# Low halves by an accumulating DMA, a single pace for the modulation items, and another filler among the attention heads

## The chip, the cores and the metric

One core of a Trainium2 chip runs one program. The time is what the device takes for one execution, in microseconds (us); the median of three runs is given. Engines are called as in the profile: PE (TensorE), PEld (its weight loads), DVE (VectorE), ACT (ScalarE), POOL (GpSimd) and SP (SyncE, which only issues DMAs here). Each engine runs its own list of instructions in order and waits at semaphores.

## What is computed

Two sequences (a prompt and a sample) of 512 tokens with D = 1024 go through the same two layers. Layer 0 mixes by retention (4 heads, scores with a decay in both directions, a gate), layer 1 by grouped-query attention (8 query heads, 2 key heads); each has an MLP of width 4096 with a squared ReLU. A conditioning vector gives six modulation vectors for each layer.

```
def adaln(c, w, b):
    mod = silu(c) @ w + b
    return split(mod, 6)                      # sh1, sc1, g1, sh2, sc2, g2

def trunk(x, c, ...):
    for i in range(2):
        sh1, sc1, g1, sh2, sc2, g2 = adaln(c, mod_w[i], mod_b[i])
        h = rmsnorm(x, norm1_g[i]) * (1 + sc1) + sh1
        m = retention(h, ...) if i == 0 else attention(h, ...)
        x = x + g1 * m
        h = rmsnorm(x, norm2_g[i]) * (1 + sc2) + sh2
        x = x + g2 * (square(relu(h @ mlp_w1[i])) @ mlp_w2[i])
    return rmsnorm(x, final_g)
```

All is fp32. mod_w is 1024 x 6144 in each layer.

## The kernel before

**Products.** A matmul operand in fp32 is split into two halves of the type f32r: hi is the value rounded, lo is the value less hi. `mm3` (L217 to 220) makes a product of three matmuls, hi·hi, hi·lo and lo·hi. Weights come in pieces of 128 x 1024 (512 KB).

**Plain pieces.** `load_piece` (L199 to 207) loads a piece into `raw` on SP's DMA queue (2 buffers), lets ACT copy it into `whi` (L205) and DVE write `wlo` as raw less whi (L206). There are 4 buffers each of whi and wlo. 174 pieces go this way: 128 in the retention (0 to 1000 us of the profiled execution), 46 in the attention (1590 to 2030 us). The two MLPs (1000 to 1590 and 2030 to 2664 us) use products of sums of blocks with their own pieces, and neither `load_piece` nor the modulation.

**Modulation.** The vectors mod are made on DVE, beside the main work. An item is one row block of mod_w for one of six chunks: two loads of 256 KB on POOL's queue (L407) and, for each sequence, two dots on DVE (L382), each a product with a running sum over 512 columns. `bg` holds items not yet loaded, `loaded` those whose loads are issued. `piece` calls `tick` after each plain piece with the instruction that the dots are to stand behind: the pace is added up, and at 1.0 one item is dotted and the next loaded. The items' tiles come from the pool f2 with 8 buffers; 6 of them are held by other things (tables of the rotation, the conditioning rows of the two sequences), so that one item with its two halves fills what is left. With `alt`, every second item takes its tiles from another pool (xf). Only the first 8 items use it before. 40 further dots, on tiles loaded by SP or with `alt`, stand ahead of these.

**Retention.** Eight steps, two sequences with four heads each; in a step PE makes scores, v, g and y, and the q, k products of the next step, in an order written out by hand (`ORDER`). Before, the first 8 items run in step 0, 16 (of one sequence) from the end of step 0 at PACE 0.55, and 8 of one sequence and 72 of both from the end of step 2 at PACE_LAST 1.0, with loops at the ends of steps 3 and 6 and a flush in step 7 that dot what has to be done by then.

**Start.** PE multiplies the first pieces while POOL computes `decay_logs` (L421 on: eleven pairs of small operations, L434 and L435, and three more) and then products for the first norm (L1174).

**Attention.** `weave` runs the heads of a sequence and takes filler from a generator `fill`, a piece at each yield: projections (p1, q2, q0) and the next sequence's norm (`nm1.steps(4)`).

Of the kernel before, what the change touches and what calls it, by code (L numbers as in the profile page):

```python
# [7 lines left out]
F32 = mybir.dt.float32  # L8
# [3 lines left out]
AF = mybir.ActivationFunctionType  # L12
ALU = mybir.AluOpType
# [5 lines left out]
EPS = 1e-6  # L19
ORDER_FIRST = "q0 q1 z0 q2 z1 z2 q3 z3"  # L20
ORDER = "g1 g2 g3 q0 z0 q1 z1 q2 z2 z3 q3"
PACE = 0.55
PACE_LAST = 1.0
SQ_W = 8
SQ_RAW = 3
SQ_SUM = 4
# [5 lines left out]
def kernel(  # L32
# [25 lines left out]
    nc = tc.nc  # L58
    act = nc.scalar.activation
    tt = nc.vector.tensor_tensor  # L60
# [6 lines left out]
    def ld(dst, src):  # L67
        ins = nc.sync.dma_start(dst, src)
        if strict[0]:
            tc.keep_in_program_order(ins)  # L70
        ld.last = ins
# [18 lines left out]
    def rtile():  # L90
        return rp.tile([P, T], F32R, tag="r", name="r")
# [39 lines left out]
    def small(w):  # L131
        return sm.tile([P, w], F32, tag=f"s{w}", name=f"s{w}")
# [13 lines left out]
    bg, loaded = [], []  # L146
    pace = [0.0, 0.0]

    def bg_dot():
        if loaded:  # L150
            f, hv = loaded.pop()
            f(hv)

    def bg_load():
        if bg:
            f, g = bg.pop(0)
            loaded.append((g, f()))

    def tick(ins):
        pace[1] += pace[0]  # L160
# [4 lines left out]
            pace[1] -= 1.0  # L165

    def flush():
        while bg or loaded:
            bg_dot()
            bg_load()  # L170

    sq = {}

# [26 lines left out]
    def load_piece(src):  # L200
        raw = rawp.tile([P, 1024], F32, tag="raw", name="raw")
        ld(raw, src)
        hi = wp.tile([P, 1024], F32R, tag="whi", name="whi")
        lo = wp.tile([P, 1024], F32R, tag="wlo", name="wlo")
        act(hi, raw, AF.Copy)  # L205
        ins = tt(lo, raw, hi.bitcast(F32), ALU.subtract)  # L206
        return hi, lo, ins

    def piece2(src, pages):
# [185 lines left out]
    def new_col(layer, ch, s):  # L395
        modc[layer, ch, s] = const.tile([P, KD], F32, name=f"mc{layer}_{ch}_{s}")

    def mod_chunk(cb, layer, ch, seqs=(0, 1), alt=False):
        accs = {s: small(2 * KD) for s in seqs}
        for s in seqs:  # L400
            new_col(layer, ch, s)

        def load(k):
            get = xtile if alt and k % 2 else f2tile
            hv = [get(), get()]
            for hf in range(2):
                nc.gpsimd.dma_start(hv[hf], modw[layer, ch * KD + k][:, hf * T:(hf + 1) * T])  # L407
            return hv

        def step(k, hv):  # L410
            for s in seqs:
                dot(accs[s], hv, cb[s], k)
            if k == KD - 1:
                for s in seqs:
                    mod_cols(accs[s], layer, ch, s, 0, KD)

        for k in range(KD):
            bg.append((lambda k=k: load(k), lambda hv, k=k: step(k, hv)))

# [677 lines left out]
    def run(g, n=None):  # L1099
        while n is None or n > 0:  # L1100
            try:
                next(g)
            except StopIteration:
                return
            if n is not None:
                n -= 1
# [15 lines left out]
    cb = [cond_row(0), None]  # L1122
# [32 lines left out]
    for i in range(4):  # L1155
        for t in range(2):
            k = 2 * i + t
# [13 lines left out]
            else:  # L1171
# [5 lines left out]
                hi, lo = rtile(), rtile()  # L1177
# [39 lines left out]
    for step in range(8):  # L1217
        s, n = divmod(step, 4)
        nm = None
        r.scores(n, strip)  # L1220
        if step == 3:
            with tc.issue_after(first_pool.ins):
                s1 = stats_of(fetch(xs[1][k]) for k in range(KD))
            nm = Norm(s1, lambda k: fetch(xs[1][k]),
                      modc[0, 1, 1], modc[0, 0, 1], True)
            r1 = Ret(1, None, nm.h)
        if step == 7:
            nm = Norm(stats_of(fetch(park[0][k]) for k in range(KD)), lambda k: fetch(park[0][k]),
                      modc[0, 4, 0], modc[0, 3, 0], True, keep=hparks[0][0])
            m.h[0] = nm.h  # L1230
        if step > 0:
            r.v(n)
        if nm is not None:
            nm.a()
        r.g(n, [0] if step else [3])
        if nm is not None:
            nm.c()
        r.y(n)
        if nm is not None:
            nm.m()  # L1240
        if step < 7:
            strip = decay_strip((n + 1) % 4)
        if step == 7:
            r.g(n, [1, 2, 3])
        if step < 7:
            nxt = r1 if step == 3 else r
            n1 = (n + 1) % 4
            for t in (ORDER if step else ORDER_FIRST).split():
                i = int(t[1])
                if t[0] == "q":  # L1250
                    nxt.qk(n1, i)
                elif t[0] == "z":
                    r.tz([i])
                else:
                    r.g(n, [i])
            if step == 0:
                flush()
                mod_chunk(cb, 0, 1, (1,))
                mod_chunk(cb, 0, 0, (1,))
                pace[0] = PACE  # L1260
            if step == 2:
                flush()
                mod_chunk(cb, 0, 2, (1,))
                for ch in (4, 3, 5):
                    mod_chunk(cb, 0, ch)
                for ch in (1, 0, 2, 3, 4, 5):
                    mod_chunk(cb, 1, ch)
                pace[0] = PACE_LAST
            if step == 3:
                while len(bg) > 71 or (loaded and len(bg) == 72):  # L1270
                    bg_dot()
                    bg_load()
            if step == 6:
                while len(bg) > 47 or (loaded and len(bg) == 48):
                    bg_dot()
                    bg_load()
            if step == 3:
                r.out(n, lambda o: nc.gpsimd.dma_start(park[0][o], x0[o]))
                r1.x = [fetch(xs[1][k], ptile) for k in range(KD)]
                r = r1  # L1280
            else:
                r.out(n)
        else:
            m.x[1] = r.x
            m.ups(0, 0, [0])
            r.tz([0, 1])
            m.ups(0, 0, [1])
            r.tz([2, 3])
            m.ups(0, 0, [2])
            st1 = Stats()  # L1290
            r.out(n, lambda o: st1.add(r.x[o]))
            with tc.issue_after(r.last.ins):
                m.x[0] = [fetch(park[0][k], ftile, nc.scalar) for k in range(KD)]
            m.ups(0, 0, [3])
            flush()
# [30 lines left out]
    nm1 = Norm(st[1], lambda k: fetch(park[1][k]), modc[1, 1, 1], modc[1, 0, 1], True)  # L1326
    a1 = Att(1, nm1.h, tabs)
    p2, p0, p1 = a0.proj(2), a0.proj(0), a0.proj(1)
# [19 lines left out]
    run(zipped(p0, p1))  # L1348

    def fill():  # L1350
        yield from p1
        yield from nm1.steps(4)
        yield from part(q2, 4)
        yield from zipped(q2, q0)

    f = fill()
    weave(a0.heads(), f)
    run(f)
# [20 lines left out]
    f = fill()  # L1379
# [21 lines left out]
    f = finish(0, st[0])  # L1401
# [159 lines left out]
```

## Time and profile before

| | us |
|---|---|
| median of 3 runs | 2667.32 |
| lowest, highest | 2665.93, 2669.35 |
| the profiled execution | 2666.18 |
| its span in the trace | 2664.4 |

The mean granted clock of PE in the profiled execution is 0.981. By stretch, PE's idle time is the length less its busy time: 23.5 us from 0 to 150, 6.8 from 150 to 430, 55.2 from 430 to 1000, 9.4 from 1000 to 1590, 20.3 from 1590 to 2030 and 20.0 to the end. A row of a timeline gives start and length; lengths of neighbours overlap, so the cost of an instruction on its engine is read from one start to the next.

### The profile page before, as it was taken

The numbers are of one execution on the slowest core, as the hardware profiler recorded it, in microseconds if no ns is written. First come the engines' busy times: TensorE is split into PE (matmuls) and PEld (weight loads), VectorE is DVE, ScalarE is ACT, GpSimd is POOL, SyncE is SP. The second block draws the span as 40 slices with busy tenths as digits, with TensorE's granted clock in tenths as the row PEclk, the third lists the DMA queues.
The fourth block names the chain that finished last, engine by engine and source line by source line (L and its number), as shares of the span: only waits on it lengthen the run. The fifth ranks groups of instructions, "written<-read, shape, count | busy, mean of one in ns | idle before, by whom it ended". The sixth has DMA issues, their size and how long they took to land. (4 is left out here: it accounts for less than half of the span.)

```text
span 2664.4 us, 32643 instructions
## 1 busy us (share of the span) xinstructions
PE 2528.7 (95%) x11186; PEld 2056.7 (77%) x11186; DVE 1991.8 (75%) x3800; ACT 1120.2 (42%) x1949; POOL 526.2 (20%) x947
## 2 busy tenths in 40 slices
PE   6999999889897999999999999899999999999998
PEld 4888887767676777888878887678778788878887
DVE  6767577778877978666778867776876766688777
ACT  3433333222222355444444434675774444454432
POOL 2302112221212212121222200000014121242100
PEclk9999999999998999999999999899999999999999
DMA  7544454644444656444565434122337454474433
GB/s 248 190 127 138 126 168 148 205 143 146 134 150 132 210 181 213 163 154 163 171 211 164 162 114 140 53 63 76 115 122 271 157 180 144 160 277 159 139 95 103
DMA packets 133994, 414.00 MB, mean 155 GB/s; under 512 B 21250, under 2 KB 24194, under 8 KB 133828
## 3 DMA queue, kind: packets, MB, share of 16 engines
q0 software_dynamic: 68352, 224.58, 24.9%
q1 hardware_dynamic: 59284, 180.32, 21.6%
q10 hardware_dynamic: 6192, 7.02, 0.8%
q8 instruction: 88, 1.44, 0.2%
q14 instruction: 78, 0.64, 0.1%
HBM read 332.15 MB, written 79.69 MB: 155 GB/s over the span
## 5 line engine op out<-in xcount | busy, mean ns | idle before, releaser
L218 PE MATMUL pm<-r,whi 128*128 128x512 f32 x768 | 306.7, 402 | 29.8 <-DVE f L572 14.6
L205 ACT ACTIVATE whi<-raw 128x1024 fp32r<-128x1024 f32 x174 | 183.6, 1057 | 339.1 <-DMA raw<-in_wri_dram 106.4
L220 PE MATMUL pm<-r,wlo 128*128 128x512 f32 x768 | 304.6, 397 | 9.1 <-DVE wlo L206 9.1
L219 PE MATMUL pm<-r,whi 128*128 128x512 f32 x768 | 305.6, 398 | 5.5 <-DVE r L313 5.4
L382 DVE SCALAR_TENSOR_TENSOR junk<-f,f 128x512 bf16<-128x512 f32 x344 | 239.6, 696 | 94.1 <-DMA f<-in_modw_dram 91.0
L206 DVE TENSOR_TENSOR wlo<-raw,whi 128x1024 fp32r<-128x1024 f32 x174 | 216.9, 1247 | 89.6 <-ACT whi L205 89.0
L225 ACT ACTIVATE wh<-rawq 128x512 fp32r<-128x512 f32 x228 | 142.5, 629 | 286.6 <-PE pm L667 159.7
L225 ACT ACTIVATE wh<-sum 128x512 fp32r<-128x512 f32 x208 | 129.9, 629 | 280.0 <-PE pa L667 178.2
L666 PE MATMUL pa<-r,wh 128*128 128x512 f32 x624 | 242.7, 389 | 0.0
L667 PE MATMUL pa<-r,wh 128*128 128x512 f32 x624 | 242.7, 389 | 0.0
L668 PE MATMUL pa<-r,wh 128*128 128x512 f32 x624 | 242.7, 389 | 0.0
L407 POOL DMA_DIRECT2D f<-in_modw_dram x200 | 108.2, 541 | 596.6 <-DVE junk L382 495.8
L218 PEld LDWEIGHTS pm<-r,whi 128*128 128x128 f32 x768 | 147.3, 192 | 65.0 <-issue 15.9
L666 PE MATMUL pm<-r,wh 128*128 128x512 f32 x468 | 182.6, 390 | 1.9 <-ACT wh L225 1.9
L668 PE MATMUL pm<-r,wh 128*128 128x512 f32 x468 | 182.1, 389 | 0.0
L667 PE MATMUL pm<-r,wh 128*128 128x512 f32 x468 | 182.1, 389 | 0.0
L220 PEld LDWEIGHTS pm<-r,wlo 128*128 128x128 f32 x768 | 147.7, 192 | 42.2 <-DVE wlo L206 11.2
L218 PE MATMUL pa<-whi,r 128*128 128x512 f32 x440 | 174.2, 399 | 5.1 <-ACT whi L205 4.2
L219 PEld LDWEIGHTS pm<-r,whi 128*128 128x128 f32 x768 | 147.9, 193 | 39.8 <-DVE r L313 8.7
L219 PE MATMUL pa<-wlo,r 128*128 128x512 f32 x440 | 174.0, 396 | 0.6 <-DVE wlo L206 0.6
L226 DVE TENSOR_TENSOR wh<-sum,wh 128x512 fp32r<-128x512 f32 x208 | 141.4, 685 | 44.1 <-ACT wh L225 42.7
L220 PE MATMUL pa<-whi,r 128*128 128x512 f32 x440 | 173.6, 394 | 0.0
(277 smaller groups left out, 5978.8 us busy)
## 6 DMA issues: line engine op xcount, KB each, us to landing
rawq<-in_w_dram SPq DMA_DIRECT2D x144, 512.0 KB, 3.9
f<-in_modw_dram POOLq DMA_DIRECT2D x200, 256.0 KB, 3.4
raw<-in_wri_dram SPq DMA_DIRECT2D x92, 512.0 KB, 3.8
r<-hhpark POOLq DMA_DIRECT2D x142, 256.0 KB, 4.1
hhpark<-f POOLq DMA_DIRECT2D x96, 256.0 KB, 2.9
hhpark<-p POOLq DMA_DIRECT2D x88, 256.0 KB, 2.3
raw<-in_wro_dram SPq DMA_DIRECT2D x32, 512.0 KB, 3.7
xf<-park POOLq DMA_DIRECT2D x48, 256.0 KB, 3.4
```

What stands on the lines that cost most here:

```text
L205: act(hi, raw, AF.Copy)
L206: ins = tt(lo, raw, hi.bitcast(F32), ALU.subtract)
L218: mm(ps, a[0], b[0], start=first, stop=False)
L219: mm(ps, a[0], b[1], start=False, stop=False)
L220: return mm(ps, a[1], b[0], start=False, stop=last)
L225: split.last = act(hi, src_f32, AF.Copy)
L226: split.dve = tt(lo, src_f32, hi.bitcast(F32), ALU.subtract)
L382: stt(junk, w[hf], 0.5, cb[hf], ALU.mult, ALU.mult, accum_out=a[:, 2 * k + hf:2 * k + hf + 1])
L407: nc.gpsimd.dma_start(hv[hf], modw[layer, ch * KD + k][:, hf * T:(hf + 1) * T])
L666: mm(ps, a[0], b[0], start=first and k == 0, stop=False, **more)
L667: mm(ps, a[0], b[1], start=False, stop=False, **more)
L668: mm(ps, a[1], b[0], start=False, stop=k == n - 1, **more)
```

## The change

Lines of the kernel after are 3 higher than those of before from L208 on (L206 is then L208 and L209, L382 is L385, L407 is L410, L434 is L437).

- `load_piece`: ACT writes −hi into wlo (the copy with scale −1), and a DMA on POOL's queue adds the piece from DRAM to it. The dots of `tick` stand behind the second copy of ACT.
- `bg_load` loads a second item ahead where its tiles are of another home than the loaded one's; dots take the oldest. `alt` is set for 32 items of layer 1.
- From the end of step 0 all 96 items run at one pace of 0.88. `bg_until(n)` dots until n items are left: 80 in step 2, 72 in step 3, 48 in step 6.
- The first filler in the attention runs p1 and the norm side by side, four yields for both, where they took their turns one after the other.

```diff
--- before.py
+++ after.py
@@ -19,8 +19,7 @@
 EPS = 1e-6
 ORDER_FIRST = "q0 q1 z0 q2 z1 z2 q3 z3"
 ORDER = "g1 g2 g3 q0 z0 q1 z1 q2 z2 z3 q3"
-PACE = 0.55
-PACE_LAST = 1.0
+PACE = 0.88
 SQ_W = 8
 SQ_RAW = 3
 SQ_SUM = 4
@@ -148,13 +147,18 @@
 
     def bg_dot():
         if loaded:
-            f, hv = loaded.pop()
+            f, hv, _ = loaded.pop(0)
             f(hv)
 
     def bg_load():
-        if bg:
-            f, g = bg.pop(0)
-            loaded.append((g, f()))
+        while bg and (not loaded or (len(loaded) == 1 and loaded[0][2] != bg[0][2])):
+            f, g, home = bg.pop(0)
+            loaded.append((g, f(), home))
+
+    def bg_until(n):
+        while len(bg) + len(loaded) > n:
+            bg_dot()
+            bg_load()
 
     def tick(ins):
         pace[1] += pace[0]
@@ -165,9 +169,7 @@
             pace[1] -= 1.0
 
     def flush():
-        while bg or loaded:
-            bg_dot()
-            bg_load()
+        bg_until(0)
 
     sq = {}
 
@@ -203,7 +205,8 @@
         hi = wp.tile([P, 1024], F32R, tag="whi", name="whi")
         lo = wp.tile([P, 1024], F32R, tag="wlo", name="wlo")
         act(hi, raw, AF.Copy)
-        ins = tt(lo, raw, hi.bitcast(F32), ALU.subtract)
+        ins = act(lo, raw, AF.Copy, scale=-1.0)
+        nc.gpsimd.dma_start(lo, src, accum_op=ALU.add)
         return hi, lo, ins
 
     def piece2(src, pages):
@@ -415,7 +418,7 @@
                     mod_cols(accs[s], layer, ch, s, 0, KD)
 
         for k in range(KD):
-            bg.append((lambda k=k: load(k), lambda hv, k=k: step(k, hv)))
+            bg.append((lambda k=k: load(k), lambda hv, k=k: step(k, hv), alt and k % 2))
 
 
 
@@ -1257,23 +1260,18 @@
                 flush()
                 mod_chunk(cb, 0, 1, (1,))
                 mod_chunk(cb, 0, 0, (1,))
-                pace[0] = PACE
-            if step == 2:
-                flush()
                 mod_chunk(cb, 0, 2, (1,))
                 for ch in (4, 3, 5):
                     mod_chunk(cb, 0, ch)
                 for ch in (1, 0, 2, 3, 4, 5):
-                    mod_chunk(cb, 1, ch)
-                pace[0] = PACE_LAST
+                    mod_chunk(cb, 1, ch, alt=ch < 4)
+                pace[0] = PACE
+            if step == 2:
+                bg_until(80)
             if step == 3:
-                while len(bg) > 71 or (loaded and len(bg) == 72):
-                    bg_dot()
-                    bg_load()
+                bg_until(72)
             if step == 6:
-                while len(bg) > 47 or (loaded and len(bg) == 48):
-                    bg_dot()
-                    bg_load()
+                bg_until(48)
             if step == 3:
                 r.out(n, lambda o: nc.gpsimd.dma_start(park[0][o], x0[o]))
                 r1.x = [fetch(xs[1][k], ptile) for k in range(KD)]
@@ -1348,8 +1346,13 @@
     run(zipped(p0, p1))
 
     def fill():
-        yield from p1
-        yield from nm1.steps(4)
+        h1 = nm1.steps(4)
+        for i in range(4):
+            run(p1, 1)
+            run(h1, 1)
+            yield
+        run(p1)
+        run(h1)
         yield from part(q2, 4)
         yield from zipped(q2, q0)
```

On DVE, in step 1 of the retention, from the last of the scores' splits to the splits of v (r is a split half, junk the unused product of a dot, f2 a half of a modulation item, wlo a low half). Before:

```order
L226 TENSOR_TENSOR r_1597<-f_1594,r_1596 128x512
L206 TENSOR_TENSOR wlo_1759<-raw_1756,whi_1758 128x1024
L206 TENSOR_TENSOR wlo_1898<-raw_1895,whi_1897 128x1024
L382 SCALAR_TENSOR_TENSOR junk_1901,s16_1396<-f2_1712,f2_923 128x512
L382 SCALAR_TENSOR_TENSOR junk_1903,s16_1396<-f2_1713,f2_928 128x512
L206 TENSOR_TENSOR wlo_1940<-raw_1937,whi_1939 128x1024
L382 SCALAR_TENSOR_TENSOR junk_1943,s16_1396<-f2_1905,f2_923 128x512
L382 SCALAR_TENSOR_TENSOR junk_1945,s16_1396<-f2_1906,f2_928 128x512
L226 TENSOR_TENSOR r_1741<-pa_1600,r_1740 128x512
L226 TENSOR_TENSOR r_1745<-pa_1601,r_1744 128x512
L226 TENSOR_TENSOR r_1749<-pa_1602,r_1748 128x512
L226 TENSOR_TENSOR r_1753<-pa_1603,r_1752 128x512
```

and after:

```order
L229 TENSOR_TENSOR r_1661<-f_1658,r_1660 128x512
L385 SCALAR_TENSOR_TENSOR junk_2172,s16_1412<-f2_2124,f2_937 128x512
L385 SCALAR_TENSOR_TENSOR junk_2239,s16_1412<-f2_2174,f2_932 128x512
L385 SCALAR_TENSOR_TENSOR junk_2241,s16_1412<-f2_2175,f2_937 128x512
L385 SCALAR_TENSOR_TENSOR junk_2301,s16_1412<-f2_2243,f2_932 128x512
L385 SCALAR_TENSOR_TENSOR junk_2303,s16_1412<-f2_2244,f2_937 128x512
L385 SCALAR_TENSOR_TENSOR junk_2394,s16_1412<-f2_2305,f2_932 128x512
L385 SCALAR_TENSOR_TENSOR junk_2396,s16_1412<-f2_2306,f2_937 128x512
L385 SCALAR_TENSOR_TENSOR junk_2437,s16_1412<-f2_2398,f2_932 128x512
L385 SCALAR_TENSOR_TENSOR junk_2439,s16_1412<-f2_2399,f2_937 128x512
L229 TENSOR_TENSOR r_1825<-pa_1664,r_1824 128x512
L229 TENSOR_TENSOR r_1829<-pa_1665,r_1828 128x512
```

Three subtractions and four dots stood between the scores and v; now nine dots stand there with no subtraction.

On POOL's list at the same place, whose rows are all DMA issues. Before:

```order
L407 DMA f2_1516<-in_modw_dram 128x512
L407 DMA f2_1517<-in_modw_dram 128x512
L407 DMA f2_1644<-in_modw_dram 128x512
L407 DMA f2_1645<-in_modw_dram 128x512
L407 DMA f2_1712<-in_modw_dram 128x512
L407 DMA f2_1713<-in_modw_dram 128x512
L407 DMA f2_1905<-in_modw_dram 128x512
L407 DMA f2_1906<-in_modw_dram 128x512
L407 DMA f2_1947<-in_modw_dram 128x512
L407 DMA f2_1948<-in_modw_dram 128x512
```

and after:

```order
L410 DMA f2_2037<-in_modw_dram 128x512
L209 DMA wlo_1749<-in_wri_dram 128x1024
L410 DMA f2_2038<-in_modw_dram 128x512
L410 DMA f2_2080<-in_modw_dram 128x512
L410 DMA f2_2081<-in_modw_dram 128x512
L209 DMA wlo_1788<-in_wri_dram 128x1024
L410 DMA f2_2123<-in_modw_dram 128x512
L410 DMA f2_2124<-in_modw_dram 128x512
L410 DMA f2_2174<-in_modw_dram 128x512
L410 DMA f2_2175<-in_modw_dram 128x512
L410 DMA f2_2243<-in_modw_dram 128x512
L209 DMA wlo_1843<-in_wri_dram 128x1024
```

The accumulates (L209) now stand between the loads of modulation halves (L410), in the order in which they are issued.

On POOL near the start, in the chain of `decay_logs` (s8 are its small tiles). Before:

```order
L435 TENSOR_SCALAR s8_686<-s8_686 128x8
L434 TENSOR_TENSOR s8_686<-s8_686,s8_688 128x8
L435 TENSOR_SCALAR s8_686<-s8_686 128x8
L434 TENSOR_TENSOR s8_686<-s8_686,s8_688 128x8
L435 TENSOR_SCALAR s8_686<-s8_686 128x8
L434 TENSOR_TENSOR s8_686<-s8_686,s8_688 128x8
```

and after:

```order
L437 TENSOR_TENSOR s8_692<-s8_692,s8_694 128x8
L438 TENSOR_SCALAR s8_692<-s8_692 128x8
L437 TENSOR_TENSOR s8_692<-s8_692,s8_694 128x8
L438 TENSOR_SCALAR s8_692<-s8_692 128x8
L209 DMA wlo_244<-in_wq0_dram 128x1024
L437 TENSOR_TENSOR s8_692<-s8_692,s8_694 128x8
L438 TENSOR_SCALAR s8_692<-s8_692 128x8
L437 TENSOR_TENSOR s8_692<-s8_692,s8_694 128x8
```

The accumulate of the first piece stands behind the seventh of the eleven pairs. Counted in the same orders on DVE, 136 dots stand ahead of the first score product of step 4 before and 225 after; of all 384, 200 and 325 stand ahead of that of step 5.

## Rows read from the trace of the kernel before

**Rows 1.** Busy time of the engines, the page's first part (us, share of the span, instructions).

```profile
PE 2528.7 (95%) x11186; PEld 2056.7 (77%) x11186; DVE 1991.8 (75%) x3800; ACT 1120.2 (42%) x1949; POOL 526.2 (20%) x947
```

**Rows 2.** Busy time by stretch: start:end, length, engines, PE clock, DMA share, GB/s.

```profile
150.00:430.00 280.00, 273.25 (x1212) 224.34 (x1211) 185.80 (x353) 84.15 (x111) 48.49 (x84) 0.99 0.47 146
430.00:1000.00 570.00, 514.76 (x2205) 413.49 (x2203) 458.28 (x1023) 173.90 (x239) 129.19 (x219) 0.96 0.50 161
...
1590.00:2030.00 440.00, 419.68 (x1943) 334.93 (x1943) 310.27 (x677) 268.72 (x593) 38.87 (x72) 0.97 0.33 102
```

**Rows 3.** What PE waited for, 430 to 1000 us: total us, times, longest.

```profile
PE pm L218 <- DVE f L572: 14.6, 3, 5.0
PE pm L220 <- DVE wlo L206: 9.1, 5, 2.3
PE pm L218 <- DVE f L533: 7.1, 2, 4.8
```

**Rows 4.** Groups by line, 430 to 1000 us: busy us, mean ns | idle before, releasers.

```profile
L382 DVE SCALAR_TENSOR_TENSOR junk<-f,f 128x512 bf16<-128x512 f32 x272 | 190.1, 699 | 78.5 <-DMA f<-in_modw_dram 76.0
...
L206 DVE TENSOR_TENSOR wlo<-raw,whi 128x1024 fp32r<-128x1024 f32 x71 | 90.6, 1277 | 11.8 <-ACT whi L205 11.6
L205 ACT ACTIVATE whi<-raw 128x1024 fp32r<-128x1024 f32 x71 | 75.1, 1057 | 151.8 <-DMA raw<-in_wri_dram 97.0 <-PE pm L219 21.5 <-DMA raw<-in_wro_dram 16.3
L407 POOL DMA_DIRECT2D f<-in_modw_dram x134 | 72.3, 540 | 338.1 <-DVE junk L382 270.8 <-DVE mc L390 25.7 <-issue 15.6
```

**Rows 5.** The same groups on DVE, 150 to 430 us.

```profile
L206 DVE TENSOR_TENSOR wlo<-raw,whi 128x1024 fp32r<-128x1024 f32 x41 | 50.6, 1234 | 44.1 <-ACT whi L205 44.0
L382 DVE SCALAR_TENSOR_TENSOR junk<-f,f 128x512 bf16<-128x512 f32 x64 | 43.9, 686 | 12.8 <-DMA f<-in_modw_dram 12.2
```

**Rows 6.** Timeline of DVE, 760 to 775 us: start, length, line, operation.

```profile
763.73 1.22 DVE L206 TENSOR_TENSOR wlo<-raw,whi 128x1024 fp32r<-128x1024 f32 x1
764.86 0.69 DVE L382 SCALAR_TENSOR_TENSOR junk<-f,f 128x512 bf16<-128x512 f32 x1
...
765.59 0.69 DVE L382 SCALAR_TENSOR_TENSOR junk<-f,f 128x512 bf16<-128x512 f32 x1
```

**Rows 7.** Timeline of POOL, 690 to 712 us.

```profile
708.07 0.54 POOL L407 DMA_DIRECT2D f<-in_modw_dram  x1 [5.35 <-DVE junk L382]
708.80 0.54 POOL L407 DMA_DIRECT2D f<-in_modw_dram  x1 [0.20 <-issue]
```

**Rows 8.** DMA issues by what they move: count, KB each, median us to landing.

```profile
f<-in_modw_dram POOLq DMA_DIRECT2D x200, 256.0 KB, 3.4
raw<-in_wri_dram SPq DMA_DIRECT2D x92, 512.0 KB, 3.8
...
f<-park POOLq DMA_DIRECT2D x24, 256.0 KB, 5.2
```

**Rows 9.** Timeline of SP, 690 to 692 us.

```profile
690.19 0.33 SPq L68 DMA_DIRECT2D raw<-in_wri_dram  x1
```

**Rows 10.** Timeline of POOL, 30 to 40 us.

```profile
33.55 0.20 POOL L435 TENSOR_SCALAR s<-s 128x8 f32<-128x8 f32 x1
...
36.86 3.73 POOL L1174 TENSOR_TENSOR rs<-p,f 128x512 f32<-128x512 f32 x3
```

**Rows 11.** Timeline of PE, 26 to 42 us.

```profile
27.51 0.63 PE L220 MATMUL pm<-r,wlo 128*128 128x512 f32 x1
...
33.23 0.40 PE L219 MATMUL pa<-wlo,r 128*128 128x512 f32 x1
33.46 0.40 PE L220 MATMUL pa<-whi,r 128*128 128x512 f32 x1
39.02 2.08 PE L218 MATMUL pm<-r,whi 128*128 128x512 f32 x4 [5.16 <-ACT r L1178]
```

**Rows 12.** What PE waited for, 1590 to 2030 us: total us, times, longest.

```profile
PE ps L218 <- ACT p L1047: 8.1, 10, 1.2
PE pa L218 <- ACT whi L205: 4.2, 1, 4.2
```

## The prediction

> **What bounds the kernel now.** I read the engines' busy shares, then each stretch, then what PE waits for where it idles. PE is the engine to feed: 2528.7 us busy of 2664.4 [rows 1]. Time can be won where PE idles or runs below full clock. From 430 to 1000 us it idles 55.2 us (570 − 514.8) at a granted clock of 0.96; from 150 to 430 it idles 6.8 us at 0.99 [rows 2]. In the first of these every larger wait of PE is for DVE [rows 3]. DVE there is busy 458.3 us and idles 76.0 us more, waiting for modulation weights [rows 2, 4]. DVE runs its list in order, so whatever follows waits too: 534 of 570 us, 94%, are taken. From 150 to 430 the same sum is 185.8 + 12.2 = 198 of 280, 71% [rows 2, 5].
>
> That gives a scale. At 71% taken PE loses 2.4% idle and about 1% by the clock, 3.4% together; at 94% it loses 9.7% and 4%, 13.7%. Between I interpolate; nothing in this trace shows DVE fuller than 94%, so above that the stretch grows until DVE fits at 94%. The work that PE must do is then 280 × 0.966 = 270 us and 570 × 0.863 = 492 us.
>
> **The change part by part.**
>
> *Subtractions.* The low half of a plain piece leaves DVE. One costs 1.13 us from its start to the next row's start [rows 6]. There are 41 in the early stretch and 71 in the late one [rows 4, 5]: −46 and −80 us of DVE. ACT gets a second 1.06 us copy for each [rows 4]; it is busy 174 of 570 us [rows 2], so I price this at nothing. In 1590 to 2030, where ACT is busy 269 of 440 us [rows 2], 46 such copies bring it to 317, still covered.
>
> *Pace.* In the order of DVE's instructions, before has 136 dots ahead of the first score product of step 4 (the fifth of eight, near the edge of the two stretches), after has 225. So 89 dots move from steps 4 to 7 into steps 0 to 3, each 0.73 us [rows 6]: 65 us of DVE leave the late stretch and enter the early one. I take the steps 1 to 3 as the early stretch and 4 to 7 as the late one; their edges differ by some 20 us.
>
> *The accumulating DMA.* Each of the 174 pieces (112 in these two stretches) gets one of 512 KB on POOL's queue, the queue that brings the modulation weights. The trace of before has no accumulate. Its issue I take as the other POOL DMAs', 0.54 us [rows 7]. Its time in the queue I bound from two copies: a 256 KB load lands 3.4 us after it is issued, of which the issue takes 0.54 [rows 7, 8], a 512 KB one 3.8 with an issue of 0.33 on SP [rows 8, 9]; 3.45 against 2.86 behind the issue are 0.6 us for each 256 KB. So 512 KB hold the engines 1.2 us as a plain copy, 2.4 us if source and destination are both read, 3.6 us if three passes count. I take 2.4, since the operation has to read both. Something cheaper than a copy is excluded, because the same bytes move; no row excludes more than 3.6. That loads in one POOL queue hold each other up is seen in the loads issued several together: f<-park lands after 5.2 us, a pair of modulation loads after 3.4 [rows 8].
>
> A load issued right behind an accumulate starts 0.73 us after it [rows 7], so it comes 2.4 − 0.73 = 1.67 us late (0.47 as a copy, 2.87 with three passes). By POOL's order in after, 40 of the 96 modulation loads of steps 1 to 3 stand directly behind an accumulate, and 30 of the 90 from step 4 on. The others meet one by chance: 112 × 2.4 us in 850 us is a share of 0.32 (0.16; 0.47), and the mean remaining hold is half the engine time less the issue, 0.7 us (0.1; 1.3). I count every such delay as DVE time, though before only 48 loads were waited for: 64 of the 96 items have one buffer pair, so their next load starts only after their dots, and the subtractions that filled the gap are gone. Only 32 items alternate between two pairs.
>
> DVE, early: 198 − 46 + 65 + 40 × 1.67 + 56 × 0.32 × 0.7 = 297 us, more than the 280 that are there. At 94% it needs 316: **+36 us**. Late: 534 − 80 − 65 + 30 × 1.67 + 60 × 0.32 × 0.7 = 452 us; with 492 us of PE work this balances at 541 us (84% taken, 9.1% lost): **−29 us**. Together +7.
>
> What this gives with the other two prices: as a copy, early 237 us (293 us long, +13), late 404 (524, −46), together −33. Three passes: early 366 (389, +109), late 512 (562, −8), together +101.
>
> The Trainium skill (Collectives: The Full Stack, "The bandwidth ceiling: the fold count and why AG ≠ RS ≠ AR") speaks against the cheap price: a reduce on the DMA engines is slow since it reads two sources, and it states 62.28 against 32.35 GB/s, a ratio of 1.93. No row here shows an accumulate. By that figure the hold would be an estimated 2.3 us instead of 2.4 and the sum some 4 us lower.
>
> *Start.* The accumulate of the first piece stands on POOL behind seven pairs of the decay chain. The seventh pair ends near 33.75 us [rows 10]. Issue 0.54, landing 3.45 and the second read 1.2 bring it to 38.9. PE wants the piece's low half at 27.51 [rows 11]. PE comes 11.4 us late into a wait of 5.16 us at 39.02 [rows 11], which takes up that much: +6 (nothing if the wait's own cause were to move earlier, +9 if POOL's multiplications at 36.86 [rows 10] also slip behind the second accumulate).
>
> *Pieces later.* A piece now takes 3.8 for the load, 2 × 1.06 for ACT and 5.2 for the accumulate, 11.1 us. PE has three others in hand, 3 × 24 matmuls × 0.23 [rows 11] = 16.3 us. POOL runs in order too: an accumulate stands behind a load that waits for its buffer's dots, 338.1 us over 67 items, 5.0 on average [rows 4]. Cover and need are then equal within 0.2 us, so a few pieces come late: I take six of 112 by a microsecond, +6 (0 to +60).
>
> *Attention.* PE already waits 4.2 us for the first piece's high half there [rows 12]; its low half now comes a second copy and an accumulate later in place of a subtraction: +4, later pieces as above. The filler spreads the next norm's work among the heads, so that more projection products stand between softmax steps. PE's waits for softmax are 8.1 us in ten [rows 12]; I take three quarters off, −6 (−8 to +5, as the norm's DVE work now stands there earlier).
>
> *Untouched.* The two wide stages use no plain pieces and no modulation: nothing.
>
> Sum: 7 + 6 + 6 + 4 − 6 = +17 us on the profiled execution's 2666.18, so 2683. The profiled execution is 1.1 us under the median of the three runs, so against it 2684.
>
> **The rivals.**
>
> *The accumulate is as cheap as a copy.* For it: queue 0 is one of several and the chip's DMA engines are only half busy (share 0.47 and 0.50 [rows 2]). Against it: it has to fetch the destination. −33, start +5, late pieces +2, attention +3 − 6, in all −29: **2637**, faster.
>
> *Three passes or a clogged queue*, the other way: +101, start +7, late pieces +20, attention +5 − 6, in all +127: **2793**. The two stretches would both be set by loads.
>
> *PE waits for the low halves themselves.* Against before, where PE's waits for wlo are 9.1 us [rows 3]: now each accumulate stands in POOL's order behind a load that waits for a dot on DVE, and that dot may stand behind a wait for PE. It decides from a POOL wait of 5.2 us on, just above the mean of 5.0. If it is twice the mean for one piece in ten, 11 pieces come 4.8 us late, +53 in place of the +6 above: **2730**, slower than before.
>
> *The change does nothing that can be told.* The DVE gain and the delay of the loads balance at about 2.2 us for the hold: **2667**. This is the lower part of the forecast's own range, 2655 to 2720.
>
> **How the numbers follow.** Two reads 0.46, a copy 0.30, three passes 0.13, PE waiting for low halves 0.11. About 0.2% (5.3 us) is what a measurement of this kernel can tell from no change. Of the 0.46, 0.10 fall below 2662, 0.09 within 2662 to 2673 and 0.27 above; of the copy's 0.30, 0.28 below and 0.02 within. So faster 0.38, same 0.11, slower 0.51. The range goes from 2630, leaving out some 0.08 of the copy's case, to 2760, leaving out some 0.11 of three passes and the worst late pieces.
>
> **What would show it.** Right: modulation loads land later than 3.4 us, above all in steps 1 to 3; DVE's wait for them from 150 to 430 grows from 12 us to some 80; PE's idle time there grows from 7 to about 35 us while that from 430 to 1000 falls below 55; DMA share rises from 0.5 to about 0.8 in both; a new PE wait for wlo's DMA near 30 us. Wrong: loads landing at 3.4 us still (the copy); PE waits for wlo's DMA all through (the third rival); PE's idle time in steps 1 to 3 unchanged, which would say that pacing costs nothing there and the whole is faster; or a change in the wide stages, which nothing here explains.

## The result and the profile after

The changed kernel takes 2755.86 us (median of 4 runs, 2750.71 to 2759.35) against 2666.62 for the kernel before in the same comparison: ratio 1.0335, 95% interval 1.0313 to 1.0356. That is 89 us slower. The side was forecast and the range held it, but the forecast was a loss of 17 us; it was wrong by a factor of five. A version with the subtraction back and every modulation item loaded two ahead (below) needs 2593 us.

The page of the changed kernel, its first, third and sixth parts (busy time; queue, packets, MB, share of 16 engines; issues with KB each and us to landing), to be read against [rows 1] and [rows 8]:

```profile
PE 2556.0 (93%) x11186; PEld 2073.1 (75%) x11186; DVE 1800.0 (65%) x3626; ACT 1277.0 (46%) x2123; POOL 674.3 (24%) x1121
...
q0 software_dynamic: 93408, 315.82, 42.5%
...
raw<-in_wri_dram SPq DMA_DIRECT2D x92, 512.0 KB, 6.3
wlo<-in_wri_dram POOLq DMA_DIRECT2D x91, 512.0 KB, 7.8
f<-in_modw_dram POOLq DMA_DIRECT2D x168, 256.0 KB, 4.3
```

and POOL's queue before:

```profile
q0 software_dynamic: 68352, 224.58, 24.9%
```

DVE lost 192 us of work, as planned, and PE still idles more. POOL's queue (q0) went from 24.9% of the span to 42.5%: 0.425 × 2757.5 − 0.249 × 2664.4 = 508 us for 174 accumulates, 2.92 us each (an estimate that takes the queue's other transfers as before). The loads of the retention land later, those of modulation (3.4 to 4.3 us) and the pieces' raw loads on SP's queue too (3.8 to 6.3 us).

Where the time went shows at marks that both kernels have: the start of the last score product's eviction of a step on DVE (L517; L520 after; a step begins with its scores), the first wide matmul and the first softmax exponential.

| mark | before | after | lost up to there |
|---|---|---|---|
| scores of step 0 | 104.2 | 114.2 | 10 |
| step 1 | 171.6 | 201.9 | 30 |
| step 2 | 276.8 | 342.8 | 66 |
| step 3 | 386.7 | 474.2 | 87 |
| step 6 | 758.8 | 875.7 | 117 |
| step 7 | 882.2 | 981.3 | 99 |
| first wide matmul | 1070.9 | 1167.2 | 96 |
| first softmax exponential | 1698.4 | 1801.4 | 103 |
| end of span | 2664.4 | 2757.5 | 93 |

So 87 us have arisen by the scores of step 3 and 30 more by those of step 6; the two last steps give some 20 back, and what comes after the retention changes the sum by 3. The stretches by engine in the changed kernel (columns as in [rows 2]), from the scores of step 1 to just short of those of step 3, and then up to the end of the retention:

```profile
201.90:473.00 271.10, 230.22 (x943) 182.89 (x943) 143.30 (x367) 93.07 (x116) 79.98 (x121) 0.93 0.78 200
473.00:1080.00 607.00, 540.58 (x2286) 436.72 (x2285) 348.53 (x836) 254.06 (x331) 180.97 (x271) 0.94 0.80 207
```

and the same in the kernel before:

```profile
171.60:386.70 215.10, 213.34 (x957) 176.46 (x956) 136.76 (x250) 64.36 (x85) 35.56 (x60) 1.00 0.44 135
386.70:980.00 593.30, 533.18 (x2276) 427.34 (x2275) 480.68 (x1086) 182.24 (x251) 139.37 (x238) 0.96 0.51 163
```

In the first of the two PE's idle time went from 1.8 to 40.9 us and its granted clock from 1.00 to 0.93, so the work itself ran slower too. DVE is busy hardly longer than before (143 against 137 us). What DVE waited for there, after (total us, times, longest):

```profile
DVE junk L385 <- DMA f<-in_modw_dram: 125.1, 56, 7.8
```

and before:

```profile
DVE junk L382 <- DMA f<-in_modw_dram: 7.0, 4, 2.4
```

PE's three largest waits in the changed kernel, from 45 to 1100 us, are for results of DVE:

```profile
PE pm L221 <- DVE p L589: 26.5, 9, 6.6
PE pa L221 <- DVE r L229: 25.0, 5, 8.2
PE pm L221 <- DVE f L575: 15.9, 6, 6.8
```

One wait of DVE and its consequence, on DVE and then on PE, step 1 of the changed kernel (timeline; the number in brackets is the idle time ahead):

```profile
229.31 0.69 DVE L385 SCALAR_TENSOR_TENSOR junk<-f,f 128x512 bf16<-128x512 f32 x1 [5.63 <-DMA f<-in_modw_dram]
...
230.69 1.28 DVE L229 TENSOR_TENSOR r<-pa,r 128x512 fp32r<-128x512 f32 x2
```

```profile
231.43 0.79 PE L221 MATMUL pa<-r 128*128 128x512 f32 x1 [7.34 <-DVE r L229]
232.03 0.63 PE L222 MATMUL pa<-r 128*128 128x512 f32 x1
232.45 0.63 PE L223 MATMUL pa<-r 128*128 128x512 f32 x1
```

DVE stands 5.63 us before a dot whose load has not landed; two splits of v stand behind it on DVE's list; PE waits 7.34 us for them, and its matmuls then start 0.42 us apart, the lower of the clock's two levels (1.2 GHz; 0.23 apart at 2.4 GHz in [rows 11]). The dot is background work: its item is not asked for before step 2 (`bg_until(80)`). It is the eighth of the nine that the order of DVE after shows between the scores' splits and the splits of v; the ninth follows at 230.07.

### The profile page after: what moved, and what is told of

Its sections match the earlier page's. It is cut to its first block, busy times and chain, and to the rows that moved or that the text cites. A ratio compares the mean times of both kernels' runs of the same rounds, so it can differ in the third digit from the quotient of the medians.

```text
span 2757.5 us, 32891 instructions
## 1 busy us (share of the span) xinstructions
PE 2556.0 (93%) x11186; PEld 2073.1 (75%) x11186; DVE 1800.0 (65%) x3626; ACT 1277.0 (46%) x2123; POOL 674.3 (24%) x1121
## 3 DMA queue, kind: packets, MB, share of 16 engines
q0 software_dynamic: 93408, 315.82, 42.5%
## 5 line engine op out<-in xcount | busy, mean ns | idle before, releaser
L385 DVE SCALAR_TENSOR_TENSOR junk<-f,f 128x512 bf16<-128x512 f32 x280 | 194.1, 693 | 255.8 <-DMA f<-in_modw_dram 252.9
L208 ACT ACTIVATE wlo<-raw 128x1024 fp32r<-128x1024 f32 x174 | 182.8, 1051 | 72.2 <-PE pa L222 66.9
L410 POOL DMA_DIRECT2D f<-in_modw_dram x168 | 98.4, 590 | 373.3 <-DVE junk L385 300.4
L228 ACT ACTIVATE r<-f 128x512 fp32r<-128x512 f32 x130 | 80.6, 629 | 206.0 <-DVE f L520 84.7
```

Source lines behind the costliest of these rows:

```text
L208: ins = act(lo, raw, AF.Copy, scale=-1.0)
L228: split.last = act(hi, src_f32, AF.Copy)
L385: stt(junk, w[hf], 0.5, cb[hf], ALU.mult, ALU.mult, accum_out=a[:, 2 * k + hf:2 * k + hf + 1])
```

## The experiments

The theory to start with: (A) the accumulates delay the loads, in POOL's order and on the DMA engines, and DVE waits for them in its list. Rival (B): the pace pulls too many dots into the early steps.

**The subtraction back, all else as changed.**

```diff
-        ins = act(lo, raw, AF.Copy, scale=-1.0)
-        nc.gpsimd.dma_start(lo, src, accum_op=ALU.add)
+        ins = tt(lo, raw, hi.bitcast(F32), ALU.subtract)
```

> The changed kernel with the DVE subtraction back in place of the second ACT copy and the accumulating DMA; the single pace, the second item ahead and the attention filler stay. Theory A (the accumulates cost the time: their hold on the DMA queue and on POOL's order makes DVE wait for modulation loads): the loss goes and the pacing's gain shows, 2635 to 2665. Theory B (the pace of 0.88 pulls too many dots into steps 0 to 3, whose DVE time was free before): DVE now has the subtractions too, so the early steps stay long, 2710 or more.

Measured 2623.56 us (2620.27 to 2626.04), ratio 0.9837 (0.9821 to 0.9853): 43 us faster than the kernel before. B falls: with the subtractions on DVE as well, the stretch from the scores of step 1 to those of step 3 takes 217.5 us, 2.4 more than before, and the gain comes after the scores of step 4. The pacing, with the second item and the filler, is a gain, larger than either theory had it, and the rest of the change costs 132 us.

**The accumulate alone, on the kernel before.** Its `load_piece` is the changed kernel's, all else is before's.

> The kernel before with only the second ACT copy and the accumulating DMA in place of the subtraction; pace, items ahead and filler as before. Theory A: most of the loss is there, 2720 to 2780, and it now falls in steps 3 to 7, where the dots are. Theory B: the early steps keep their length and the whole stays within 2640 to 2680.

2775.61 us, ratio 1.0410 (1.0389 to 1.0431): 109 us slower. The cost comes with the new `load_piece` under either pacing. The place that A expected was wrong: already at the scores of step 2 this kernel is at 345.9 us, like the changed one (342.8), with the slow pace there.

**A plain copy in place of the accumulate.**

```diff
-        nc.gpsimd.dma_start(lo, src, accum_op=ALU.add)
+        nc.gpsimd.dma_start(lo, src)
```

> The changed kernel, but the DMA behind the second ACT copy is a plain copy of the same 512 KB into the same tile, with no accumulate, so the low half is the piece itself and the result is wrong; issue, order and waits stay. Theory A1: the hold falls from 2.9 us (the growth of queue 0's share over 174 accumulates) to about 1.7 (the SP queue's time for 512 KB), and with it some 50 to 60 us of the loss: 2690 to 2710. Theory A2: as the changed kernel, 2740 or more.

2682.10 us (2680.45 to 2683.74). This is the cleanest comparison of all, since each engine's list has the same rows in the same order as in the changed kernel. The adding alone costs 73.8 us, more than A1's 50 to 60. The copy's queue and issues:

```profile
q0 software_dynamic: 93408, 315.82, 35.0%
...
wlo<-in_wri_dram POOLq DMA_DIRECT2D x91, 512.0 KB, 5.2
f<-in_modw_dram POOLq DMA_DIRECT2D x168, 256.0 KB, 3.9
...
raw<-in_wri_dram SPq DMA_DIRECT2D x92, 512.0 KB, 4.5
```

A copy holds the engines 0.350 × 2678.6 − 663.4 = 274 us, over 174 of them 1.58 us; the accumulate's 2.92 are 1.85 times that. It also takes POOL longer to issue. First the accumulate in the changed kernel, then the copy, both over the whole span (groups by line: busy us, mean ns | idle before, releasers):

```profile
L209 POOL DMA_DIRECT2D wlo<-in_wri_dram x91 | 83.5, 922 | 137.5 <-ACT wlo L208 133.6 <-DMA f<-in_modw_dram 1.9 <-ACT f L535 1.6
```

```profile
L209 POOL DMA_DIRECT2D wlo<-in_wri_dram x91 | 49.8, 548 | 151.0 <-ACT wlo L208 145.3 <-DMA f<-in_modw_dram 4.8 <-DMA xf<-park 0.4
```

0.92 against 0.55 us. How much of the 73.8 us is the hold and how much the issue, this pair doesn't separate; the runs that follow allow an estimate.

**Smaller accumulates**, of 64 and of 512 columns (`lo[:, 0:64]`, `src[:, 0:64]`, and so on).

> The changed kernel, but each accumulating DMA moves 64 of the 1024 columns (32 KB in place of 512 KB), so the low halves are left wrong in the other columns; issue, order on POOL and the wait for ACT's second copy stay. Theory A1 (the transfer's hold on the DMA engines): the loss goes, 2620 to 2660, and DVE's wait for modulation loads from step 0 to step 6 falls from 260 us to about 100. Theory A2 (POOL's order: the accumulate waits for ACT's second copy, 112 us in all, and the loads behind it start late): nearly all stays, 2720 or more, with DVE's wait above 200 us.

> The changed kernel with accumulates of 512 of the 1024 columns (256 KB each; the other half of each low half is left wrong). If the loss grows with the time that accumulates hold the DMA engines in a straight line between 32 KB (2674.7) and 512 KB (2755.9): 2712. If it sets in only when the engines are nearly full (DMA share 0.8 in steps 0 to 6): 2680 to 2695.

2674.71 us (8 runs, 2669.06 to 2677.87) and 2720.85 us (2717.44 to 2724.26). Neither A1 nor A2 alone holds for the first: some 81 of the 132 us go with the bytes, 51 stay without them, and DVE's wait for modulation loads (160 us) lies between the two theories' numbers. The half one lies a little above the straight line (2712), so nothing speaks for a threshold at a full queue. In both the scheduler placed a few hundred of DVE's 3626 rows otherwise than in the changed kernel, so that they are bounds and no exact dose. One thing they show well: 256 KB accumulated hold the engines 0.344 × 2722.3 − 663.4 = 273 us in all, 1.57 each, the time of 512 KB copied.

**No DMA at all.**

> The changed kernel without the accumulating DMA at all: the second ACT copy stays and leaves the negated high half in the low half's place, so the result is wrong. Theory A2a (POOL's order costs the 51 us between the 64-column accumulate and the subtraction: loads wait behind an accumulate that waits for ACT): about 2610 to 2630. Theory A2b (ACT's order costs them: the second copy waits for a free low-half buffer and the splits behind it on ACT come late, so DVE waits): about 2665 to 2680, as with the 64-column accumulate.

2661.38 us (6 runs, 2657.05 to 2669.36). Of the 51 us, 38 stay with no accumulate on POOL; POOL's order is worth the smaller part, 13. These 13 hold all that the issue of 174 accumulates costs as well, since those of 32 KB took as long to issue (0.92 us) as those of 512 KB. So by these runs the longer issue can explain some 13 of the 73.8 us between accumulate and copy, and the rest goes with the bytes; as the orders differ, this is an estimate and not a measurement. The number is 4 us under A2b's range and far from A2a's. A2b's cause did not hold:

**ACT's second copy beside the subtraction.**

```diff
+        act(lo, raw, AF.Copy, scale=-1.0)
         ins = tt(lo, raw, hi.bitcast(F32), ALU.subtract)
```

> The kernel with the subtraction back, and the second ACT copy as well (into the low half, which the subtraction then overwrites): ACT's list is that of the changed kernel, DVE's that with the subtractions, and there is no DMA on POOL. Theory C1 (ACT's order: the second copies hold up the splits behind them): about 2660, as the changed kernel without its DMA. Theory C2 (the subtractions gone from DVE's list: they stood between the dots and gave the loads time): about 2624 to 2635.

2624.33 us (2621.99 to 2626.67) against 2623.56 without the copy: ACT's copies cost nothing that can be told. So the 38 us came from the subtraction's absence from DVE's list. There are two ways in which a subtraction can help, and one column of it tells them apart.

**A tie of one column in place of the subtraction**, without the DMA, and then in the changed kernel.

```diff
-        ins = act(lo, raw, AF.Copy, scale=-1.0)
+        act(lo, raw, AF.Copy, scale=-1.0)
+        tie = small(1)
+        ins = tt(tie, raw[:, 0:1], hi[:, 0:1].bitcast(F32), ALU.subtract)
```

> The changed kernel without its DMA (low halves left wrong, as in the run without the accumulate at 2661.4) plus a subtraction of one single column on DVE that waits for ACT's first copy, with the dots tied to it as they were to the whole subtraction. Theory D1 (what the subtraction gave was the tie: it held a dot on DVE's list until its piece had come): about 2600 to 2630, DVE's wait for modulation loads down from 164 us to 60 or 80. Theory D2 (what it gave was time between the dots, 1.13 us each, in which the next load lands): 2655 to 2670, the wait stays above 140.

> The changed kernel with its accumulates and the same one-column subtraction as a tie for the dots. Theory D1: 2700 to 2725, some 38 us less than the changed kernel. Theory D2, or if the accumulates' hold on the DMA engines covers everything: 2745 to 2760.

2605.94 us (2605.90 to 2605.98) and 2722.77 us (2720.43 to 2725.11). D1 holds in the first: an instruction of 0.2 us, on which the dots are hung, is worth 55 us. DVE's wait for modulation loads and for the tie in it, and then for modulation loads without it, 0 to 1000 us:

```profile
L386 DVE SCALAR_TENSOR_TENSOR junk<-f,f 128x512 bf16<-128x512 f32 x280 | 192.9, 689 | 84.7 <-DMA f<-in_modw_dram 81.0
L210 DVE TENSOR_TENSOR s<-raw,whi 128x1 f32<-128x1 f32 x130 | 26.0, 202 | 109.8 <-ACT whi L207 109.7
```

```profile
L384 DVE SCALAR_TENSOR_TENSOR junk<-f,f 128x512 bf16<-128x512 f32 x280 | 195.6, 699 | 167.3 <-DMA f<-in_modw_dram 163.7
```

The wait did not vanish, it moved: DVE now stands 109.7 us at the tie. But PE waits less for it: it is busy 951.5 of these 1000 us, without the tie 923.0. The order shows it at the place that was shown ahead of the prediction. With the tie, on DVE, from the last of the scores' splits to the splits of v (timeline; the small rows of the dots' ends and of the modulation vectors are left out):

```profile
168.34 1.48 DVE L230 TENSOR_TENSOR r<-f,r 128x512 fp32r<-128x512 f32 x2
174.58 0.16 DVE L210 TENSOR_TENSOR s<-raw,whi 128x1 f32<-128x1 f32 x1 [4.76 <-ACT whi L207]
180.02 0.16 DVE L210 TENSOR_TENSOR s<-raw,whi 128x1 f32<-128x1 f32 x1 [5.28 <-ACT whi L207]
180.10 0.69 DVE L386 SCALAR_TENSOR_TENSOR junk<-f,f 128x512 bf16<-128x512 f32 x1
...
180.83 0.69 DVE L386 SCALAR_TENSOR_TENSOR junk<-f,f 128x512 bf16<-128x512 f32 x1
...
185.46 0.16 DVE L210 TENSOR_TENSOR s<-raw,whi 128x1 f32<-128x1 f32 x1 [3.94 <-ACT whi L207]
185.54 0.69 DVE L386 SCALAR_TENSOR_TENSOR junk<-f,f 128x512 bf16<-128x512 f32 x1
...
186.28 0.69 DVE L386 SCALAR_TENSOR_TENSOR junk<-f,f 128x512 bf16<-128x512 f32 x1
...
187.63 2.05 DVE L230 TENSOR_TENSOR r<-pa,r 128x512 fp32r<-128x512 f32 x3 [0.17 <-ACT r L229]
```

Four dots and three ties, as four dots and three subtractions before; the changed kernel has nine dots in that place. Counted in the traces over all steps, these dots stand on DVE ahead of the first score product's eviction of step 4:

| kernel | dots |
|---|---|
| before | 136 |
| changed | 225 |
| accumulates alone, old pace | 228 |
| subtraction back, new pace | 177 |
| no DMA, no tie, new pace | 233 |
| no DMA, tie, new pace | 180 |

So less than half of the 89 dots that moved forward came with the new pace; the others slipped ahead because nothing on DVE's list held them to a piece, and under the old pace they did so too. The second run says that this carries over: the tie takes 33 us off the changed kernel. D1's 2700 to 2725 just holds. With the tie in both, the accumulates cost 2722.8 − 2605.9 = 117 us.

**Every item two ahead, with accumulates and with subtractions** (`alt=True` at every chunk).

> The changed kernel, accumulates and all, with every modulation chunk alternating between the two homes, so that all 96 items are loaded two ahead. Theory A (DVE's in-order waits for loads that come late carry the loss): most of it goes, 2640 to 2680, and DVE's wait for modulation loads falls from 260 us to below 80. If the accumulates cost by themselves (PE waits for low halves, raw loads late): 2720 or more.

> The kernel with the subtraction back, and every modulation chunk alternating between the two homes of tiles, so that a second item is ahead in all 96 and not in 32. If DVE's remaining wait for modulation loads (56 us) is what keeps PE waiting in the retention: 2605 to 2618. If the third tile of the other pool is missed by the main work: 2624 or more.

2712.57 us and 2593.36 us (2589.43 to 2596.24; ratio 0.9724, 0.9705 to 0.9742). Neither lies in a range that was named. The second beats both kernels: 73 us less than before, 162 less than the changed kernel. There DVE waits 11 us in all for modulation loads. With accumulates a second item takes off 43 us but not the loss, and DVE still waits 125 us for these loads; 119 us remain between the two. From 0 to 1150 us with accumulates the clock is 0.95 and the DMA share 0.81; over the first 1000 us with subtractions:

```profile
0.00:1150.00 1150.00, 1023.57 (x4317) 823.78 (x4318) 699.79 (x1643) 489.21 (x651) 352.98 (x553) 0.95 0.81 217
```

```profile
0.00:1000.00 1000.00, 955.85 (x4171) 779.30 (x4171) 814.56 (x1739) 354.96 (x497) 236.16 (x413) 0.98 0.55 177
```

DVE is fuller in the fast kernel (81% busy) than in the slow one (61%), also with its waits for modulation loads counted in (83% and 72%).

**The modulation loads on SP's queue**, with the accumulates left alone on POOL's.

> The changed kernel with the modulation loads on SP's queue, so that POOL's queue holds the accumulates without them. If the loads are late because they stand behind accumulates and their waits on POOL: 2690 to 2710. If the DMA engines are simply full, or if the piece loads now wait on SP behind loads that wait for dots: 2750 or more, with PE waiting for pieces.

2733.64 us: 22 us less than the changed kernel. Neither number came. Standing behind accumulates in one queue is part of the loss; how large a part stays open, since the move has a price of its own. ACT's waits for the pieces' loads (raw from `in_wri`, ahead of its first copy) grow from 21.9 to 60.9 us. On the other queue the modulation loads still land after 4.2 us and DVE waits 203 us for them.

**The pacing without the second item, and the old filler**, both with the subtraction.

> The kernel with the subtraction back and the single pace, but with every item of the 96 in one home, so that none is loaded two ahead. If the single pace (89 dots moved ahead of step 4) is what gives the 43 us: 2625 to 2635. If the second item ahead gives it: 2650 to 2665.

> The kernel with the subtraction back, the single pace and the second item ahead, and with the attention filler of the kernel before. If the filler is worth the 6 us of the prediction: 2629 to 2631 against 2623.6. If all of the gain is the pacing's: 2624; the attention stretch would then be as long as with the new filler.

2647.51 us (2645.75 to 2649.84) and 2625.08 us (2622.85 to 2626.89). The single pace gives 19 us and the second item for 32 of the 96 another 24; so both of the first run's alternatives were half right. With the subtraction on DVE the new pace moves 41 dots ahead of step 4 and not the 89 of the expectation. The filler's 1.5 us are within the spread.

Put in one chain, each step one of these runs:

| | us | step |
|---|---|---|
| before | 2666.6 | |
| single pace (and filler) | 2647.5 | −19 |
| a second item ahead for 32 items | 2623.6 | −24 |
| subtraction off DVE, dots still tied to pieces | 2605.9 | −18 |
| the tie gone | 2661.4 | +55 |
| 512 KB copies on POOL's queue | 2682.1 | +21 |
| accumulates in place of copies: the changed kernel | 2755.9 | +74 |

The order in which the parts are taken matters somewhat (the tie is worth 33 us with accumulates, 55 without). In every step but the last the scheduler also gives DVE another order; the last is the only one that changes nothing but the DMA.

## Why the prediction was right in sign and wrong in size

The kind of the loss was foreseen: modulation loads that land late behind accumulates, DVE that waits for them, a DMA share of 0.78 and 0.80. The size was not, and the right side owes something to luck: two losses were taken too small, and a gain of 43 us from pace and second item, which by the prediction's own scale is nothing, hid part of them. That the range held 2755.86 us is owed to its end at 2760. That end stood for three passes and the worst late pieces; the hold came out between two reads and three passes (2.92 us), and late pieces cost little.

*The start* came near. PE's wait for the first low half was put at 11.4 us; the changed kernel's timelines of POOL and PE have

```profile
32.01 0.97 POOL L209 DMA_DIRECT2D wlo<-in_wq_dram  x1
```

```profile
39.74 1.65 PE L223 MATMUL pm<-r,wlo 128*128 128x512 f32 x3 [10.82 <-DMA wlo<-in_wq_dram]
```

and step 0's scores come 10 us late, against +6 in the sum: the accumulate in POOL's list behind the decay chain, as read. Two misses cancel in it: the issue came at 32.0 us and not at 33.75, and the low half 7.7 us after it and not 5.2.

*ACT at nothing* was right, as the run with both copy and subtraction shows.

*The subtractions* are the step that failed first. The prediction took 46 and 80 us off DVE's demand and turned demand into time by the scale "71% taken loses 3.4%, 94% loses 13.7%". By that scale the pacing without any accumulate should have changed nothing: early 198 + 65 = 263 us, 302 long (+22); late 534 − 65 = 469, 547 long (−23). It gained 43, of which the second item ahead, for which the sum has no term, is 24. And the fastest kernel here has DVE at 81% busy, a slow one at 61%. What counts is not how full DVE is but what stands on its list ahead of an urgent split. The prediction had the evidence in its own order: nine dots in a row ahead of v's splits, where four had stood. It counted the subtraction as work only; on DVE's list it was also what kept a background dot from going ahead of its piece. That was worth 55 us without accumulates, 33 with them. The step *Pace* took the 89 dots for the pace's doing; 48 of them came from the missing tie.

*The stretches.* The prediction took 150 to 430 us for steps 1 to 3. But the scores of step 4 begin at 506.8 us in the kernel before, so that 65 us of dots were put into a stretch that ends 77 us too early. Cut at the same matmuls as 150, 430 and 1000 us in [rows 2], the changed kernel has

```profile
170.30:525.20 354.90, 297.05 (x1211) 235.64 (x1210) 186.30 (x475) 121.24 (x152) 102.82 (x157) 0.92 0.78 199
525.20:1096.00 570.80, 517.87 (x2204) 419.56 (x2203) 327.39 (x768) 238.94 (x310) 166.72 (x248) 0.95 0.80 207
```

The early stretch grew by 75 us, not 36, the late one by 1 in place of shrinking by 29. DVE's busy time and its waits for modulation loads (148.4 and 87.6 us) make 335 and 415 us, where the sum had 297 and 452: in the late stretch DVE had less to do than foreseen, and PE still lost more.

*The accumulate's price.* Taken: 2.4 us of hold, 0.54 of issue, landing after 5.2. Measured: 2.92, 0.92 and 7.8. The case of the copy was put at 2637 and the case of two reads at 2684, 47 apart; measured in one order, copy and accumulate are 74 apart. The kind was right (an accumulate holds the engines 1.85 times as long as a copy of the same bytes), the size too small: the factor of two stood on 1.2 us, the difference of two landings, and a 512 KB copy on this queue holds the engines 1.58 us. With 2.92 us put in, the sum's own formula gives 345 and 549 us for the two stretches, by my estimate +54 in all in place of +17, still short of 89. The figure of the Trainium skill (Collectives: The Full Stack, "The bandwidth ceiling: the fold count and why AG ≠ RS ≠ AR"), 1.93 between copying and reducing, agrees in kind with this 1.85. That the raw loads on SP would share the engines and go from 3.8 to 6.3 us had no term. In the rival that balances at 2.2 us of hold the two stretches do balance, but start, pieces, attention and filler add 10, so that it stood at about 2675 and not at 2667.

*The other loads.* The sum let a load suffer only behind an accumulate or by chance meeting one. With the loads on another queue 22 us of the loss went, no more. DVE's wait in the early stretch was forecast at some 80 us and came to 148, PE's idle time there at 35 and came to 57.9; the clock fell from 0.99 to 0.92 as well.

*Late pieces* were +6 and are about that: PE's waits for low halves after the start come to 11.7 us in the retention, where PE waited 9.1 us for DVE's low halves before, so the third rival falls.

*Attention.* Up to the first softmax the stretch lost 6.7 us (forecast +4), with one wait of 9.8 us for the first low half; the heads took 260.2 us for 269.3. That difference of 9 looked like the filler's −6; with the subtraction back the filler gives 1.5 us, which can't be told from nothing, so the heads' gain in the changed kernel isn't shown to be the filler's.

What stays open: how exactly the 74 us between copy and accumulate divide between the hold on the engines and POOL's longer issue (some 13 us at most, by the runs with small accumulates), and how much of the accumulates' loss comes by their place in POOL's queue and how much by the DMA engines that are busy with them.

## What to carry to other kernels

Before an instruction is taken off an engine, look at what its wait does for the order: a short operation that waits for a piece also holds background work back, and if it goes, that work needs another tie (0.2 us of one gave 55 us here). A second buffer for background loads was worth more here than an engine with less to do: with it in all items the kernel with the subtractions gained 54 us (2647.5 to 2593.4), and DVE's wait for these loads fell from 93 to 11 us. An accumulating DMA saves an engine's time at the price of nearly two copies on the DMA engines: with these already half busy, the loads on SP's queue and on POOL's came later.

## What the runs showed of the hardware that was not expected

An accumulating DMA of 512 KB took 0.92 us to issue on POOL, and one of 32 KB as long (0.92), against 0.55 for a copy in the same place, and 2.92 us of the sixteen DMA engines against 1.58. It landed 7.8 us after its issue, the copy 5.2. An accumulate of 256 KB held the engines as long as a copy of 512 KB (1.57 and 1.58 us).
